# First tokens three weight blocks ahead in the output projection, and the FFN's first weight block done for 128 tokens at a time

## Chip, core and metric

The kernel runs on one core of a Trainium2 chip. The metric is the device time of one execution in microseconds (us); lower is better. Times are the median of several runs. The profile and the trace are of one further execution, whose span (first to last instruction) is a little shorter than its time.

## What is computed

One transformer layer over 256 latent tokens of width 2048 with 256 context tokens. The change concerns the step from the first half of the layer to the second. In the reference:

```
y = (sigmoid(ga) * (oa @ w_br_a) + sigmoid(gb) * (ob @ w_br_b)) @ w_o
x = x + gt1 * rms_norm(y, g_attn_post)
h = modulate(rms_norm(x, g_ffn_pre), sh2, sc2)          # h * (1 + sc2) + sh2
u = depthwise_conv(h @ w_up, conv_w, conv_b)            # w_up: 2048 x 11264
a, g = split(u, 2)
x = x + gt2 * rms_norm((silu(g) * a) @ w_down, g_ffn_post)
```

So the projection `@ w_o` must be complete over all 2048 columns of a token before that token's norm is known, and all of `h` follows from two such norms, one after the other. Between the last product of the projection and the first of the FFN lies a passage of small steps.

## The kernel before

Weights come from HBM in blocks of 128 x 2048 (`raw`, four buffers, loaded by SyncE's queue in one fixed order). `split` makes two float32r halves of each block, a high one on ScalarE (line 127, `wh`) and the rest on VectorE (line 131, `wl`); a block is split in two pieces of 1024 columns. Each product is done as three matmuls, high by high, high by low and low by high. `block()` hands out the next block, splits the one after it and loads further ones.

**The projection** (`norm_gain`, called with `nm="o"`) holds its weights as the moving operand: four column groups `c` of 512, each four blocks deep. Tokens are in two halves, t = 0 (first 128) and t = 1 (the others), with one PSUM tile each, `py_o..0` and `py_o..1`. In the last column group both halves share the first blocks, then the last `lead` = 2 blocks are done for t = 0 first and, with the same weights held, for t = 1. `close(t)` squares and sums the result on ScalarE and multiplies it by a gain on VectorE; `residual(t)` (the argument `done`) takes the norm, adds to `x1`, and takes the second norm's sum of squares. For t = 1 the last 512 columns of `x1` are also made on TensorE, in PSUM (`px`, lines 979 and 985, with a diagonal matrix `dg` of the norm's factor).

**The passage.** `scaled(t, c0, c1)` multiplies feature tiles c0 to c1 of `x1` by the second norm's factor into `yg` (VectorE, or ScalarE with a last argument True). `turn(b, ts)` transposes the feature tiles of group b for the token halves ts on TensorE into the PSUM tile `ptx` b. `split_h2(b)` makes from it the two float32r parts of `h2` for each feature tile j: the high one on ScalarE (line 1043), the low one on VectorE (lines 1047 and 1048; for every fourth j ScalarE does one more pass, line 1042, and VectorE one fewer, line 1045). `keep_busy` issues matmuls whose result nobody uses.

**The FFN's first weight blocks** are laid out so that four output tiles `pu` 0 to 3 grow together over the 16 feature tiles k: `first_pairs(k)` issues for each of the four one matmul of 512 columns (line 174) and one of 256 (line 175). Block `B_UP` holds k = 0 to 3, the next one k = 4 to 7, and so on. Afterwards the FFN goes output tile by output tile.

The order on TensorE is as written in the passage (`manual_schedule`); on the other engines a scheduler sets it, bound by `issue_after`. Each engine runs its instructions in order, and semaphores join the engines. A PSUM tile is used by one engine at a time: where two feature tiles share one `ptx`, ScalarE's read of the second waits for VectorE's read of the first.

## Time and profile before

| | before |
|---|---|
| time, median of 3 runs | 1512.99 us (1512.9 to 1513.67) |
| time of the profiled execution | 1512.95 us |
| its span | 1511.0 us |
| TensorE busy | 1499.6 us, 99% of the span |
| VectorE, ScalarE busy | 1132.4 us (75%), 781.6 us (52%) |
| mean granted TensorE clock | 0.999 of full speed |

TensorE's matmuls are pipelined: a busy engine is one with a matmul in flight, and what one matmul costs is the distance from its start to the next one's start. All starts are in us from the span's start.

### The profile page before, as it was taken

The page shows a single profiled execution, that of the slowest core. Times are in us where ns is not written, and L with a number is a line of the kernel's source. Part 1 is how long each engine was busy: PE and PEld are TensorE (multiplying, and loading weights), DVE is VectorE, ACT ScalarE, POOL GpSimd, SP SyncE. Part 2 cuts the span into 40 slices and gives each one's busy share as a digit, 9 for nine tenths or more (in the row PEclk, how much of TensorE's full clock was granted, in tenths as well). Part 3 has the DMA queues.
Part 4 walks back from the last instruction along what each step waited for, and adds up shares of the span by engine and source line. Part 5 has one row for each costly group of instructions (what it writes and reads, how often), then busy time and mean ns, then how long its engine had stood idle before and what let it go on. Part 6 is the DMA issues. An engine that isn't in the chain of part 4 may idle for free.

```text
span 1511.0 us, 21644 instructions
## 1 busy us (share of the span) xinstructions
PE 1499.6 (99%) x8549; PEld 1289.3 (85%) x8549; DVE 1132.4 (75%) x1679; ACT 781.6 (52%) x1277; POOL 1.6 (0%) x10
## 2 busy tenths in 40 slices
PE   9999999999999999999999999999999999999998
PEld 7876889898888888888888888888888888888886
DVE  4496997999988888877678888788788776444444
ACT  4342542777764455554467555555555555344342
POOL 0000000000000000000000000000000000000000
PEclk9999999999999999999999999999999999999999
DMA  9988779754368888879846676666666556555552
GB/s 368 401 319 335 273 290 341 263 168 168 140 252 294 324 327 308 309 268 356 309 178 226 249 250 220 238 243 236 234 248 232 192 192 257 217 195 195 195 195 84
DMA packets 59253, 381.07 MB, mean 252 GB/s; under 512 B 6544, under 2 KB 6928, under 8 KB 17040
## 3 DMA queue, kind: packets, MB, share of 16 engines
q1 hardware_dynamic: 58432, 378.63, 67.5%
q8 instruction: 67, 1.10, 0.3%
q10 hardware_dynamic: 720, 1.07, 0.2%
q14 instruction: 34, 0.28, 0.1%
HBM read 375.43 MB, written 4.24 MB: 251 GB/s over the span
## 4 chain that ended last, share of the span: by engine, by line
PE 97%; DVE 1%; DMA 1%; ACT 1%; issue 0%; DVEq 0%; ACTq 0%
PE pu L174 21%; PE py_d L883 16%; PE pu L175 11%; PE pv L656 7%; PE pg L174 7%; PE pk L438 7%; PE py_o L883 6%; PE pq L174 4%; PE pb L174 4%; PE pg L175 4%; PE pq L175 2%; PE pb L175 2%; PE s L763 1%; PE po L793 1%; PE pm L312 1%; PE pt L784 1%
## 5 line engine op out<-in xcount | busy, mean ns | idle before, releaser
L131 DVE TENSOR_TENSOR wl<-raw,wh 128x1024 fp32r<-128x1024 f32 x444 | 529.9, 1221 | 222.8 <-ACT wh L127 222.7
L127 ACT ACTIVATE wh<-raw 128x1024 fp32r<-128x1024 f32 x444 | 452.9, 1054 | 294.6 <-PE py_d L883 129.2
L174 PE MATMUL pu<-h,wh 128*128 128x512 f32 x1404 | 488.1, 391 | 0.0
L175 PE MATMUL pu<-h,wl 128*128 128x256 f32 x1404 | 395.9, 282 | 0.0
L174 PEld LDWEIGHTS pu<-h,wh 128*128 128x128 f32 x1404 | 263.6, 188 | 55.6 <-issue 0.4
L175 PEld LDWEIGHTS pu<-h,wl 128*128 128x128 f32 x1404 | 265.4, 189 | 0.0
L883 PE MATMUL py_d<-wh,ff 128*128 128x512 f32 x704 | 216.8, 389 | 0.0
L174 PE MATMUL pg<-h,wh 128*128 128x512 f32 x464 | 161.5, 390 | 0.0
L883 PEld LDWEIGHTS py_d<-wh,ff 128*128 128x128 f32 x704 | 132.1, 188 | 27.6
L204 DVE SCALAR_TENSOR_TENSOR raw<-raw,crb 128x2048 f32<-128x2048 f32 x64 | 146.2, 2285 | 8.8 <-DMA raw<-in_wm_b_dram 8.7
L883 PE MATMUL py_d<-wl,ff 128*128 128x512 f32 x352 | 136.9, 389 | 0.0
L175 PE MATMUL pg<-h,wl 128*128 128x256 f32 x464 | 130.8, 282 | 0.0
L438 PE MATMUL pk<-h,ku 128*128 128x512 f32 x480 | 118.1, 398 | 0.9 <-DVE ku L131 0.4
L179 ACT ACTIVATE half_u<-pu 128x256 f32<-128x256 f32 x88 | 33.5, 383 | 152.7 <-PE pu L175 152.7
L438 PEld LDWEIGHTS pk<-h,ku 128*128 128x128 f32 x480 | 87.5, 188 | 25.6 <-issue 4.8
L174 PE MATMUL pq<-h,wh 128*128 128x512 f32 x304 | 108.6, 395 | 0.0
L174 PEld LDWEIGHTS pg<-h,wh 128*128 128x128 f32 x464 | 87.1, 188 | 18.2
L656 PE MATMUL pv<-wh,h 128*128 128x512 f32 (+1 forms) x384 | 101.8, 354 | 0.0
L174 PE MATMUL pb<-h,wh 128*128 128x512 f32 x256 | 89.4, 390 | 0.0
L175 PEld LDWEIGHTS pg<-h,wl 128*128 128x128 f32 x464 | 87.7, 189 | 0.0
L175 PE MATMUL pq<-h,wl 128*128 128x256 f32 x304 | 85.5, 281 | 0.0
L180 DVE TENSOR_TENSOR u<-pu,half_u 128x256 f32<-128x256 f32 x88 | 37.1, 423 | 56.7 <-ACT half_u L179 56.6
(193 smaller groups left out, 1790.4 us busy)
## 6 DMA issues: line engine op xcount, KB each, us to landing
raw<-in_ws_dram SPq DMA_DIRECT2D x222, 1024.0 KB, 4.8
raw<-in_wm_b_dram SPq DMA_DIRECT2D x64, 1024.0 KB, 4.9
raw<-in_wm_sc_dram SPq DMA_DIRECT2D x15, 1024.0 KB, 7.4
raw<-in_wm_sh_dram SPq DMA_DIRECT2D x16, 768.0 KB, 6.8
raw<-in_wkt_dram SPq DMA_DIRECT2D x10, 1024.0 KB, 5.1
raw<-in_wk_dram SPq DMA_DIRECT2D x7, 768.0 KB, 8.0
crb<-sild SPq DMA_DIRECT2D x5, 1024.0 KB, 6.4
sd<-in_wm_sd_dram SPq DMA_DIRECT2D x4, 1024.0 KB, 8.1
```

The source lines that it names most:

```text
L127: a_ = nc.scalar.activation(hi, src, AF.Copy)
L131: v_ = nc.vector.tensor_tensor(out=lo, in0=src, in1=hi, op=ALU.subtract)
L174: nc.tensor.matmul(pt[:, :], wh[:, w], a, start=first and i == 0, stop=False, skip_group_check=True)
L175: nc.tensor.matmul(pt[:, :S], wl[:, w], a[:, 0], start=False, stop=last and i == n - 1, skip_group_check=True)
L179: a_ = nc.scalar.activation(t[:], pt[:, S:], AF.Copy)
L180: v_ = nc.vector.tensor_tensor(out=out_, in0=pt[:, :S], in1=t[:], op=ALU.add)
L204: nc.vector.scalar_tensor_tensor(out=r, in0=r, scalar=1.0, in1=row, op0=ALU.mult, op1=ALU.mult, accum_out=modx[:, j : j + 1])
L312: nc.tensor.matmul(pm[32 * j : 32 * j + 32, t * P : t * P + P], cc[:, q, :], rsc[k + t][:, q * P : q * P + P], start=q < 4, stop=q >= KT - ...
L438: nc.tensor.matmul(pk[:], wt[:, w], hh[:, :, k, a], start=k == 0 and a == 0 and wt is wh, stop=k == KT - 1 and a == 1)
L656: nc.tensor.matmul(pv[i][:, :nw], src[:, k, a, t0 : t0 + P], wt[:, w], start=k == 0 and q == 0, stop=k == KT - 1 and q == 2)
L763: nc.tensor.matmul(s_ps[:], qs[hd][:, a, qt * P : qt * P + P], k_, start=q == 0, stop=q == 2)
L883: p_ = nc.tensor.matmul(py[t][:], act[:, k, a, t * P : t * P + P], wt[:, w], start=k == 0 and q == 0, stop=k == nk - 1 and q == 2)
```

## The change

In the last column group of the projection `lead` becomes 3, so the first tokens are done three blocks ahead of the others. That needs a third place for split weights: block `B_UP - 2` goes into the second half of `h2`, which is not yet in use, and the half of block `B_UP + 1` that serves k = 4 and 5 is split early into `crt`, the tile of a row that is no longer needed. The other half keeps its place in the passage.

While the others' last block is being done (after the first of its four k), four transposes are put between its matmuls (`ahead(1)`): feature tiles 0 to 3 of the first tokens, in two PSUM tiles `a` and `b`. Their `h2` is made at once, and `close(1)` stands behind it on ScalarE and VectorE.

`half_pairs(k, t)` does the FFN's first weight block (k = 0 to 3) for one token half: for each of the four `pu` one matmul of 2 x 128 columns and one of 128 (or, for k = 0 and t = 1, three of 128). For t = 0 it runs in the passage, two k ahead of the second half of `px` and two behind, in the place of most of `keep_busy`. For t = 1 it runs after the passage, in the place of `first_pairs(0)` to `first_pairs(3)`. `first_pairs` goes on from k = 4. The groups of feature tiles are cut anew: tiles 1 to 3 of the second tokens share one PSUM tile, and from tile 4 on they go in pairs (4, 5), (6, 7) and so on, where before they were (1, 2), (3, 4), (5, 6) and on. The first tokens' transposes of the second norm are all made from `yg`, after `scaled`, where before the first seven were made with a diagonal matrix.

```diff
-    def norm_gain(act, nk, yg, grow, ss, nm, lead, done, extra=None):
+    def norm_gain(act, nk, yg, grow, ss, nm, lead, done, extra=None, ahead=None):
...
-            py = [acc(f"py_{nm}{c}_{t}") for t in range(2)]
+            py, before = [acc(f"py_{nm}{c}_{t}") for t in range(2)], []
...
-            def part(wts, g, t):
+            def part(wts, g, t, between=None):
                 wh, wl = wts
                 for kk in range(4):
+                    if between and kk == 1:
+                        between()
                     k = 4 * g + kk
                     w = slice(kk * 512, kk * 512 + 512)
                     for q, (a, wt) in enumerate(((0, wh), (1, wh), (0, wl))):
...
             def close(t, after=None):
                 with ExitStack() as es:
-                    if after:
-                        es.enter_context(tc.issue_after(after))
+                    for i_ in [after] * bool(after) + before:
+                        es.enter_context(tc.issue_after(i_))
                     nc.scalar.activation(yg[:, t, cs], py[t][:], AF.Square, accum_out=ss[:, t, c : c + 1])
-                nc.vector.tensor_tensor(out=yg[:, t, cs], in0=py[t][:], in1=grow[:, cs], op=ALU.mult)
+                    nc.vector.tensor_tensor(out=yg[:, t, cs], in0=py[t][:], in1=grow[:, cs], op=ALU.mult)
...
                     wts.append(block(3))
                     part(wts[-1], g, 0)
-                for t in range(2):
-                    if t:
-                        for i, g in enumerate(range(n - lead, n)):
-                            part(wts[i], g, 1)
-                    close(t, after)
-                    after = done(t)
+                if ahead:
+                    ahead(0)
+                with ExitStack() as es:
+                    for t in range(2):
+                        if t:
+                            es.enter_context(tc.issue_after(final[0]))
+                            es.enter_context(tc.manual_schedule(engines={mybir.EngineType.PE}))
+                            for i, g in enumerate(range(n - lead, n)):
+                                part(wts[i], g, 1, (lambda: before.extend(ahead(1))) if ahead and i == lead - 1 else None)
+                        close(t, after)
+                        after = done(t)
         return after
...
-        crb = silu_row(yp)
+
+        crt = yp.tile([P, D], F32R, name="crt")
+        crb = crt[:].bitcast(F32)
+        sync.dma_start(out=crb, in_=sild[:KT].rearrange("a b -> (a b)").partition_broadcast(P))
...
+        tail = h2[:, KT // 2 :].rearrange("p k a s -> p (k a s)")
+        place[b0 + B_UP - 2] = (tail[:, :2048], tail[:, 2048:])
         place[b0 + B_UP - 1] = yp
...
+        def half_pairs(k, t, part=0):
+
+
+            ts = slice(t * P, t * P + P)
+            wh, wl = parts[nb_[0]]
+            for i in range(4):
+                w = slice(k % 4 * 512 + i * P, k % 4 * 512 + i * P + P)
+                both = pu[i][:].rearrange("p (a s) -> p a s", a=2)[:, :, ts]
+                if part == 0:
+                    nc.tensor.matmul(
+                        both, wh[:, w], h2[:, k, :, ts], start=k == 0 and t == 0, stop=False, skip_group_check=True)
+                    nc.tensor.matmul(pu[i][:, ts], wl[:, w], h2[:, k, 0, ts], start=False, stop=False, skip_group_check=True)
+                elif part == 1:
+                    for wt in (wh, wl):
+                        nc.tensor.matmul(
+                            pu[i][:, ts], wt[:, w], h2[:, k, 0, ts], start=False, stop=False, skip_group_check=True)
+                else:
+                    nc.tensor.matmul(
+                        pu[i][:, S + t * P : S + t * P + P], wh[:, w], h2[:, k, 1, ts], start=False, stop=False,
+                        skip_group_check=True)
...
-                pu.extend(acc(f"pu0_{i}") for i in range(4))
-                px = pu[3]
-                with tc.issue_after(final[0]):
-                    p_ = nc.tensor.matmul(px[:], ident[:], x1[:, t, c3], start=True, stop=False).ins
-                with tc.issue_after(p_):
-                    b_ = keep_busy(4, "2", pu[0])
-                with tc.issue_after(diagonal(0, t)):
-                    diagonal(1, 0)
-                with tc.issue_after(b_):
-                    p_ = nc.tensor.matmul(px[:], dg[0][:], yg[:, t, c3], start=False, stop=True).ins
+                px = acc("px")
+                nc.tensor.matmul(px[:], ident[:], x1[:, t, c3], start=True, stop=False)
+                dg[0] = yp.tile([P, P], F32, name="dg0")
+                nc.scalar.activation(dg[0][:], ident[:], AF.Copy, scale=r[:, 0, t : t + 1])
+                half_pairs(0, 0)
+                half_pairs(1, 0)
+                p_ = nc.tensor.matmul(px[:], dg[0][:], yg[:, t, c3], start=False, stop=True).ins
...
-                if t and c == 2:
+                if c == (2 if t else 3):
...
             if t == 0:
                 rstd_tok(ss[:, 1, t], r[:, 1, t : t + 1])
+                scaled(0, 0, 4)
                 return a_.ins
             with tc.issue_after(v_.ins), tc.issue_after(a_.ins):
-                return p_, rstd_tok(ss[:, 1, t], r[:, 1, t : t + 1])[0]
-
-        p_, q_ = norm_gain(zz, KT, yg, grow, ss[:, 0], "o", 2, residual, beside)
-        zs.close()
-
-
-        group = [(0,)] + [(j, j + 1) for j in range(1, KT - 1, 2)] + [(KT - 1,)]
+                return p_, rstd_tok(ss[:, 1, t], r[:, 1, t : t + 1])[0], px
...
+        group = {"a": (0, 1), "b": (2, 3), 0: (0,), 1: (1, 2, 3)}
+        group.update({2 + i: (4 + 2 * i, 5 + 2 * i) for i in range(6)})
...
-                ptx[b] = (acc if b % 2 else bank)(f"ptx{b}")
+                ptx[b] = (acc if b in (2, 3, 5, 7) else bank)(f"ptx{b}")
+            n = S if b in range(2, 8) else P
             for t in ts:
...
-                        nc.tensor.matmul(d, x1[:, t, j * P : j * P + P], dg[1][:], start=True, stop=True)
-                    else:
-                        nc.tensor.transpose(d, yg[:, t, j * P : j * P + P], ident[:])
-
-        def split_h2(b):
+                    o = f * n + (t * P if n == S else 0)
+                    nc.tensor.transpose(ptx[b][:, o : o + P], yg[:, t, j * P : j * P + P], ident[:])
...
+        def split_h2(b, *args):
             with ExitStack() as es:
                 for i_ in behind:
                     es.enter_context(tc.issue_after(i_))
-                behind[:] = split_tiles(b)
+                behind[:] = split_tiles(b, *args)
             return behind
...
+        nb_ = [0]
+        t0, t1 = slice(0, P), slice(P, S)
+
+        def ahead(i):
+            if i == 0:
+                nb_[0] = nblk[0]
+                pu.extend(acc(f"pu0_{i}") for i in range(4))
+                r_ = raws[nb_[0] + 1]
+                with tc.issue_after(last[0]), tc.issue_after(last[1]):
+                    split(crt[:, : D // 2], crt[:, D // 2 :], r_[:, : D // 2])
+            else:
+
+                for b in "ab":
+                    turn(b, (0,))
+                for j in range(4):
+                    split_h2("ab"[j // 2], t0, (j,))
+                scaled(0, 4, 8)
+                return behind[:]
+
+        p_, q_, px = norm_gain(zz, KT, yg, grow, ss[:, 0], "o", 3, residual, beside, ahead)
+        zs.close()
...
+        def first_pairs(k):
+
+            wts = (crt[:, : D // 2], crt[:, D // 2 :]) if k in (4, 5) else (wh, wl)
...
+                mm2(pu[i], *wts, h2, k % 4, 1, k, False, k == KT - 1, step=512, off=i * P)
 
         wh, wl = parts[nblk[0]]
         with tc.issue_after(p_), tc.manual_schedule(engines={mybir.EngineType.PE}):
-            for b in range(4):
+            half_pairs(2, 0)
+            half_pairs(3, 0)
+            for b in (2, 3):
                 turn(b, (0,))
-            keep_busy(8, "3", pu[0])
-
-            a_ = nc.scalar.activation(x1[:, 1, 1536:], pu[3][:], AF.Copy)
-            with tc.issue_after(a_.ins), tc.issue_after(q_):
-                scaled(0, 7, 8, True)
-                scaled(0, 8, 12, True)
+            ptx[0] = bank("ptx0")
+            keep_busy(3, "3", ptx[0])
+
+            nc.scalar.activation(x1[:, 1, 1536:], px[:], AF.Copy)
             scaled(1, 0, 1)
             scaled(1, 1, 4)
-            scaled(1, 4, 8)
-            behind[:] = [scaled(1, 8, 12)]
+            behind[:] = [q_, scaled(1, 4, 8)]
             turn(0, (1,))
-            split_h2(0)
+            split_h2(0, t1)
             turn(1, (1,))
-            first_pairs(0, 1)
-            split_h2(1)
+            half_pairs(0, 1, 1)
+            split_h2(1, t1, (1,))
+            half_pairs(0, 1, 2)
+            split_h2(1, t1, (2, 3))
+            half_pairs(1, 1)
             turn(2, (1,))
-            first_pairs(0, 2)
-            queue[nblk[0] + 1] = split_h2(2)[:]
+            split_h2(2)
+            half_pairs(2, 1)
+            turn(3, (1,))
+            queue[nblk[0] + 1] = behind[:]
             block(3)
             behind[:] = last
-            turn(3, (1,))
-            first_pairs(1)
+            with tc.issue_after(behind[0]):
+                behind[0] = scaled(0, 8, 12, True)
+            half_pairs(3, 1)
             split_h2(3)
+            with tc.issue_after(behind[1]):
+                behind[1] = scaled(1, 8, 12)
             with tc.issue_after(behind[0]):
                 behind[0] = scaled(0, 12, 16, True)
-            with tc.issue_after(behind[1]):
-                behind[1] = scaled(1, 12, 16)
-            for k in range(2, KT):
+            for k in range(4, KT):
                 if k % 4 == 0:
                     wh, wl = parts[nblk[0]]
-                b = {5: 4, 7: 5, 8: 6, 10: 7, 12: 8}.get(k)
+                b = {5: 4, 7: 5, 9: 6, 11: 7}.get(k)
                 if b:
                     turn(b, (0, 1))
                     split_h2(b)
-                    if b % 2 == 0:
-                        queue[nblk[0] + 1] = behind[:]
-                        block(3)
+                    if b == 4:
+                        with tc.issue_after(behind[1]):
+                            behind[1] = scaled(1, 12, 16)
+                if k in (5, 9, 12):
+                    queue[nblk[0] + 1] = behind[:]
+                    block(3)
+                    behind[:] = last
                 first_pairs(k)
             for q in range(2):
                 sync.dma_start(out=x1d[:, q], in_=x1[:, q])
```

The change moves instructions at three places. **TensorE at the projection's end.** Before (L883 is the projection, `py_o_1` the second tokens' sum, L979 and L985 make `px` in `pu_3`, L236 is `keep_busy`, L1025 the first tokens' transposes):

```order
L883 MATMUL py_o_1_6901<-wh_6966,zz 128x512 x2
L883 MATMUL py_o_1_6901<-wl_6967,zz 128x512
L979 MATMUL pu_3_7057<-x_6466,ident 128x512 [waits DMAHW4_49]
L236 MATMUL pu_0_7054<-ident 128x128 x4
L985 MATMUL pu_3_7057<-yg,dg_7063 128x512 [waits Activation_49]
L1025 MATMUL ptx_7082<-dg_7065,x_6466 128x128 [waits DMAHW6_49,Activation_49]
```

With the change (L890 is the projection, L1053 a transpose, `ptxa` and `ptxb` the first tokens' tiles 0 to 3, `h_6462` in the first row the weights that lie in `h2`):

```order
L890 MATMUL py_o_1_6901<-h_6462,zz 128x512 x12
L890 MATMUL py_o_1_6901<-wh_6952,zz 128x512 x2
L890 MATMUL py_o_1_6901<-wl_6953,zz 128x512
L1053 MATMUL ptxa<-ident,yg 128x128 [waits DVE_49]
L1053 MATMUL ptxa<-ident,yg 128x128
L1053 MATMUL ptxb<-ident,yg 128x128 x2
L890 MATMUL py_o_1_6901<-wh_6952,zz 128x512 x2
```

Four transposes, the first of which waits for VectorE, now stand in front of the projection's last nine matmuls.

**VectorE after the second norm of the second tokens.** Before (L925 ends the norm's factor, L969 is `scaled`: feature tile 0, tiles 1 to 3, 4 to 7 and 8 to 11; L1047 and L1048 make a low part of `h2`):

```order
L925 RECIPROCAL r<-r 128x1 [waits Activation_49]
L969 TENSOR_SCALAR yg<-x_6466,r 128x128 [waits DVE_49]
L969 TENSOR_SCALAR yg<-x_6466,r 128x384
L969 TENSOR_SCALAR yg<-x_6466,r 128x512 x2
L1047 TENSOR_SCALAR h2t_7109<-h_6462,modx 128x256 [waits Activation_49]
L1048 SCALAR_TENSOR_TENSOR h_6462<-ptx_7082,gcol,h2t_7109 128x256 [waits DVE_49,PE_49]
```

With the change (L1069, L1070 and L1067 make low parts, of tile 3 for the second tokens in the first two rows and then of tiles 4 to 7, L131 splits weights, L982 is `scaled` for tiles 8 to 11):

```order
L1069 TENSOR_SCALAR h2t_128_7179<-h_6462,modx 128x128 [waits Activation_49]
L1070 SCALAR_TENSOR_TENSOR h_6462<-ptx_7155,gcol,h2t_128_7179 128x128 [waits DVE_49]
L1069 TENSOR_SCALAR h2t_0_7193<-h_6462,modx 128x256 [waits Activation_49]
L1070 SCALAR_TENSOR_TENSOR h_6462<-ptx_7136,gcol,h2t_0_7193 128x256 [waits DVE_49,PE_49]
L1069 TENSOR_SCALAR h2t_0_7197<-h_6462,modx 128x256 [waits Activation_49]
L1070 SCALAR_TENSOR_TENSOR h_6462<-ptx_7136,gcol,h2t_0_7197 128x256 [waits DVE_49]
L131 TENSOR_TENSOR wl_7212<-raw_6958,wh_7211 128x1024 [waits Activation_49]
L1069 TENSOR_SCALAR h2t_0_7226<-h_6462,modx 128x256 [waits Activation_49]
L1070 SCALAR_TENSOR_TENSOR h_6462<-ptx_7139,gcol,h2t_0_7226 128x256 [waits DVE_49,PE_49]
L1067 TENSOR_TENSOR h_6462<-h2t_0_7230,h_6462 128x256 [waits Activation_49]
L982 TENSOR_SCALAR yg<-x_6466,r 128x512
L1069 TENSOR_SCALAR h2t_0_7249<-h_6462,modx 128x256 [waits DVE_49,Activation_49]
```

`scaled` for tiles 8 to 11 of the second tokens stood in front of all the low parts; now it stands behind those of tiles 0 to 7 and behind half a weight block.

**TensorE around k = 4 and 5.** Before (L174 and L175 are `first_pairs`, k = 4 ahead of the transposes L1027 and k = 5 behind them):

```order
L174 MATMUL pu_3_7057<-h_6462,wh_7145 128x512
L175 MATMUL pu_3_7057<-h_6462,wl_7146 128x256
L1027 MATMUL ptx_7197<-ident,yg 128x128 [waits PE_49]
L1027 MATMUL ptx_7197<-ident,yg 128x128 x3
L174 MATMUL pu_0_7054<-h_6462,wh_7145 128x512 [waits DVE_49,Activation_49]
```

With the change (L179 and L180 are `first_pairs`, L1053 the transposes of tiles 8 and 9, first tokens, then second):

```order
L179 MATMUL pu_3_6995<-h_6462,crt 128x512
L180 MATMUL pu_3_6995<-h_6462,crt 128x256
L1053 MATMUL ptx_7244<-ident,yg 128x128 [waits Activation_49]
L1053 MATMUL ptx_7244<-ident,yg 128x128
L1053 MATMUL ptx_7244<-ident,yg 128x128 [waits DVE_49]
L1053 MATMUL ptx_7244<-ident,yg 128x128
L179 MATMUL pu_0_6992<-h_6462,crt 128x512
```

The transposes of tiles 8 and 9 for both token halves stand between k = 4 and k = 5 as before (there they were of tiles 7 and 8), but the third of them now waits for VectorE, whose work for it is the L982 row above.

## Rows read from the trace of the kernel before

**Rows 1.** The page: busy time by engine, and the chain that ended last.

```profile
PE 1499.6 (99%) x8549; PEld 1289.3 (85%) x8549; DVE 1132.4 (75%) x1679; ACT 781.6 (52%) x1277; POOL 1.6 (0%) x10
...
PE 97%; DVE 1%; DMA 1%; ACT 1%; issue 0%; DVEq 0%; ACTq 0%
```

**Rows 2.** Stretches: length, busy us of each engine (instructions), clock, DMA.

```profile
765.20:772.60 7.40, 6.73 (x46) 5.32 (x44) 5.58 (x15) 6.08 (x18) 0.00 (x0) 1.00 0.51 215
772.60:798.00 25.40, 25.37 (x155) 22.36 (x155) 20.91 (x37) 17.25 (x28) 0.00 (x0) 1.00 0.44 164
798.00:1268.00 470.00, 470.00 (x2709) 416.43 (x2708) 374.05 (x554) 272.07 (x434) 0.00 (x0) 1.00 0.63 227
1503.60:1507.80 4.20, 0.00 (x0) 0.00 (x0) 3.45 (x6) 0.98 (x3) 0.00 (x0) 1.00 0.35 134
1507.90:1511.00 3.10, 0.00 (x0) 0.00 (x0) 0.00 (x0) 0.00 (x0) 0.00 (x0) 0.50 0.51 194
```

**Rows 3.** Timeline of TensorE: start, us, then the instruction; the passage.

```profile
759.78 0.62 PE L883 MATMUL py_o<-wh,zz 128*128 128x512 f32 x2
...
765.22 1.02 PE L979 MATMUL pu<-x,ident 128*128 128x512 f32 x2
...
767.39 1.12 PE L985 MATMUL pu<-yg,dg 128*128 128x512 f32 x2 [0.26 <-ACT dg L962]
768.35 1.72 PE L1025 MATMUL ptx<-dg,x 128*128 128x128 f32 x14
769.91 1.95 PE L236 MATMUL pu<-ident 128*128 128x128 f32 x16
771.70 0.49 PE L1027 MATMUL ptx<-ident,yg 128*128 128x128 f32 x3
772.63 0.39 PE L1061 MATMUL pu<-h,wh 128*128 128x256 f32 x1 [0.44 <-ACT h L1043]
```

**Rows 4.** Timeline of VectorE and ScalarE: the norms of both token halves.

```profile
759.98 0.60 ACT L892 ACTIVATE yg<-py_o 128x512 f32<-128x512 f32 x1 [3.65 <-PE py_o L883]
...
761.50 2.74 DVE L988 SCALAR_TENSOR_TENSOR x<-yg,r,x 128x512 f32<-128x512 f32 x4
...
765.42 0.60 ACT L892 ACTIVATE yg<-py_o 128x512 f32<-128x512 f32 x1
...
766.93 0.69 ACT L962 ACTIVATE dg<-ident,r 128x128 f32<-128x128 f32 x2 [0.50 <-DVE r L925]
...
769.04 0.69 DVE L994 SCALAR_TENSOR_TENSOR yg<-x 128x512 f32<-128x512 f32 x1
...
770.85 1.41 DVE L969 TENSOR_SCALAR yg<-x,r 128x128 f32<-128x128 f32 x4
```

**Rows 5.** Timeline of ScalarE and VectorE: the parts of `h2`, tiles 0 to 7.

```profile
772.01 1.02 ACT L1043 ACTIVATE h<-ptx,modx,gcol 128x256 fp32r<-128x256 f32 x2 [0.49 <-PE ptx L1027]
...
776.40 0.35 DVE L1047 TENSOR_SCALAR h2t<-h,modx 128x256 f32<-128x256 f32 x1
...
777.34 2.36 DVE L131 TENSOR_TENSOR wl<-raw,wh 128x1024 fp32r<-128x1024 f32 x2
...
780.08 0.48 DVE L1048 SCALAR_TENSOR_TENSOR h<-ptx,gcol,h2t 128x256 fp32r<-128x256 f32 x1
780.60 0.56 ACT L1043 ACTIVATE h<-ptx,modx,gcol 128x256 fp32r<-128x256 f32 x1 [1.88 <-DVE h L1048]
781.58 0.48 DVE L1048 SCALAR_TENSOR_TENSOR h<-ptx,gcol,h2t 128x256 fp32r<-128x256 f32 x1
781.99 0.48 DVE L969 TENSOR_SCALAR yg<-x,r 128x512 f32<-128x512 f32 x1
782.71 0.43 DVE L1045 TENSOR_TENSOR h<-h2t,h 128x256 fp32r<-128x256 f32 x1 [0.25 <-ACT h L1043]
```

**Rows 6.** Timeline of TensorE: transposes before k = 5, its start, the first blocks' end.

```profile
780.29 0.60 PE L1027 MATMUL ptx<-ident,yg 128*128 128x128 f32 x4
780.71 0.47 PE L174 MATMUL pu<-h,wh 128*128 128x512 f32 x1
...
797.65 0.39 PE L174 MATMUL pu<-h,wh 128*128 128x512 f32 x1
797.88 0.28 PE L175 MATMUL pu<-h,wl 128*128 128x256 f32 x1
798.00 0.39 PE L174 MATMUL pu<-h,wh 128*128 128x512 f32 x1
```

More of the change, by code (lines that the diff above doesn't have):

```diff
@@ L132, in split, with halves @@
         return a_.ins, v_.ins
[L134 removed]
+    def halves(r, off, pool=None, after=None, first=0):
         n = r.shape[-1]
         b = 1 if pool else 2
[L137 to L140 removed]
+        if isinstance(pool, tuple):
+            h, lo = pool
+        else:
+            h, lo = (
+                (pool or wp).tile([P, 2048 + 128], F32R, tag=f"w{q}", bufs=b, name=f"w{q}{nraw[0]}")[:, off : off + 2048]
+                for q in "hl")
+        for q in (slice(0, n // 2), slice(n // 2, n))[first:]:
             last[:] = split(h[:, q], lo[:, q], r[:, q], after)
@@ L159, in split_to @@
             if q not in parts:
-                parts[q] = halves(raws[q], 8 if q - b0 < B_Q else 0, place.get(q), queue.get(q))
+                parts[q] = halves(
+                    raws[q], 8 if q - b0 < B_Q else 0, place.get(q), queue.get(q), int(q == b0 + B_UP + 1))
     def block(ahead=2, split=True):
@@ L1053, in first_pairs @@
-        def first_pairs(k, part=0):
-            for i in range(4):
-                w = slice(k % 4 * 512 + i * P, k % 4 * 512 + i * P + P)
-                if part == 0:
-                    mm2(pu[i], wh, wl, h2, k % 4, 1, k, False, k == KT - 1, step=512, off=i * P)
-                elif part == 1:
-                    for q, wt in enumerate((wh, wl)):
-                        nc.tensor.matmul(pu[i][:, :S], wt[:, w], h2[:, k, 0], start=q == 0, stop=False, skip_group_check=True)
-                else:
-                    nc.tensor.matmul(pu[i][:, S:], wh[:, w], h2[:, k, 1], start=False, stop=False, skip_group_check=True)
+        nb_ = [0]
```

48 lines of the change are left out of this document (20 added, 28 removed).

## The prediction

> **What bounds the kernel now.** I began with the page: TensorE has a matmul in flight for 99% of the span, and the chain that ended last is 97% TensorE [rows 1]. So a microsecond more or less on TensorE, anywhere, is a microsecond of the time, as long as nothing later has slack. The stretches say where slack is left: behind the first weight blocks the FFN runs 470.00 us with TensorE busy for all 470.00 of them, so whatever the passage loses or gains arrives at the end unchanged [rows 2]. What is to be had lies in the passage, 765.2 to 772.6. Its rows show real work (the two halves of `px`, the first tokens' transposes) and fillers, 16 of them from 769.91 to 771.70 [rows 3]. In the stretch behind it, 772.6 to 798.0, TensorE is busy for 25.37 of 25.40 us, but VectorE is too for 20.91 [rows 2]: it feeds TensorE there with little to spare. That is the number that I kept in mind.
>
> **Prices.** The last 24 matmuls of the projection take 759.78 to 765.22, 0.227 us each for 512 columns; fourteen transposing matmuls take 768.35 to 769.91, 0.111 each [rows 3]. In `first_pairs` a matmul of 512 columns takes 0.23 and one of 256 takes 0.12, so a whole k (four of each) 1.39 [rows 6]. A float32r matmul of 128 columns stands in no row. The bounds are 0.06 (half of 256 columns) and 0.22 (twice the plain float32 rows' 0.111). I take 0.11, since those rows are the only ones of 128 columns.
>
> **Step 1, the projection's end: +1.2 us.** With three blocks held back, 36 matmuls (8.16 us) stand behind the first tokens' last one, which therefore ends at 757.06 instead of 759.78. Their `close` follows 0.20 later, as before, and the adds of the residual end 4.26 later, at 761.52 (759.98 to 764.24) [rows 4]. Then come a square on VectorE, the norm's factor and `scaled`; the same steps of the second tokens take 1.81 us from start to `scaled` (769.04 to 770.85) [rows 4], and `scaled` of 512 columns takes 0.48 [rows 5]. So the four new transposes can begin at about 763.9. TensorE reaches them after 27 of its 36 matmuls, at 763.18. It waits 0.7 us with the projection's last nine matmuls behind it; the transposes add 0.44. The projection ends at 766.4 instead of 765.22.
>
> The third block held, and the half block split into `crt`, cost nothing that I can see: ScalarE stood idle for 3.65 us in front of the first `close` [rows 4], and the block that goes into `h2` need not wait for a buffer, so these splits move into earlier idle time. If that cover were missing, the first `close`, and all behind it, would slip by as much as the half's split takes, about 1.2 us (half of 2.36) [rows 5]. SyncE's queue has the same order as before. The raw buffer of block `B_UP + 1` comes free about 2 us later, and the block that takes its place is due only after the first blocks.
>
> **Step 2, the second tokens' `close`: another +1.2.** It now stands behind the four first-token tiles on both ScalarE and VectorE. How long such a tile takes is read where two share a PSUM tile: ScalarE idles 1.88 us until VectorE is done with the one (780.56), starts at 780.60, and VectorE ends the second at 782.06, so 1.50 us for a tile of 256 columns [rows 5]. For 128 columns no row exists; it lies between 0.75 (half) and 1.50. I take 1.1, since the two hand-overs and the fixed part of three instructions do not shrink. From 764.35 three such tiles and ScalarE's part of the fourth bring the second `close` to 767.8; before it began at 765.42 [rows 4]. With 0.75 it would be 766.8, with 1.50 about 769.
>
> **Step 3, up to the second tokens' first tile: +2.0 in all.** `scaled` follows the `close` by 5.43 us (765.42 to 770.85) [rows 4], now at 773.25. TensorE has its own queue until then: from 766.4, `px` in two parts of 0.96 (767.39 to 768.35) [rows 3], 32 matmuls of `half_pairs` at 0.115 (3.7), four transposes, six fillers (0.7), and about 0.6 of waiting for `dg`, which is ready 1.86 us after the `close` (766.93 plus half of 0.69) [rows 4]. That ends at 773.7. ScalarE's first tile follows by 0.31 (771.70 to 772.01) [rows 3, 5], at 774.0, where before it stood at 772.01. What the change wanted out of the passage, half of the work of k = 0 to 3, is done by now, but 2.0 us later than the passage ended before.
>
> **Step 4, the wait ahead of k = 5: +2.5.** This is the largest term. The transposes of tiles 8 and 9 need `scaled` of tiles 8 to 11, which on VectorE has moved from in front of all low parts to behind those of tile 7. I add up the chain from 774.0. Tiles 0 to 3 of the second tokens, three of them in one PSUM tile: 4.3 (four whole tiles with one such hand-over took 772.01 to 776.40, 4.4). Tile 4: 0.94 (776.40 to 777.34). Tile 5, waiting for tile 4: 1.50. Half a weight block: 1.18 (half of 2.36). Tile 6: 0.9. Tile 7, whose two passes on ScalarE (1.02 together) wait for tile 6, with VectorE's 0.43 behind: 1.5. `scaled`: 0.48. All from [rows 5]. Together 10.8, so the third transpose starts at 784.9 and k = 5 at 785.2. Before, it started at 780.71 [rows 6], 8.70 after the first tile. On TensorE there is meanwhile only the second tokens' 36 half matmuls (4.1), four transposes (0.4) and k = 4 (1.4); it arrives at about 780.6 and waits some 4.2 us, with two transposes in the middle. Sum so far: 785.2 - 780.7 = +4.5.
>
> **Step 5, from k = 5 on: +0.5.** Eleven k as before (780.71 to 798.00 with everything between) [rows 6], two transposes fewer (-0.2). VectorE leaves step 4 with all of tiles 8 to 15 and two and a half weight blocks still to do, pairs again one behind the other: up to the first half of the weights of k = 12 that is about 12 us (tiles 8 to 13 at 0.94 and 1.5 in turn, three halves at 1.18, `scaled`, and some waiting), against some 11 of TensorE's work. I put 0.7 for waits there.
>
> **Sum.** +4.5 + 0.5 = +5.0 on the profiled execution's 1512.95 (span 1511.0 and some 2 us around it; it stands at the median of the runs, 1512.99): **1518.0 us**. The price of the 128-column matmul hardly enters: at 0.06 TensorE only waits longer for VectorE, and at 0.22 part of its 40 x 0.11 = 4.4 more falls into waits, for about +7.3 in all. With tiles of 0.75 the sum is about +3.6, with tiles of 1.50 about +7.4.
>
> **Rivals.**
> *VectorE keeps up, and TensorE's own work decides (the other side).* From 766.4 TensorE has `px` 1.9, the first weight block in halves 7.8, twelve k 16.7, 27 transposes 3.0 and fillers 0.7, in all 30.1: the first blocks end at 796.5 instead of 798.0. That is -1.5, 1511.4 us, no change that can be measured; faster only if a 128-column matmul costs 0.06, which takes off another 40 x 0.05 = 2.0 to 2.2 (1509.3). It decides once the chain of step 4 is under about 6.5 us instead of 10.8. For it speaks that four of the chain's eight tiles are half as wide; against it that VectorE's own work in that chain, without any hand-over, comes to 6.3 to 7.9 us (four tiles at half or all of 0.83, three at 0.83, then 0.43, 1.18 and 0.48, all [rows 5]), and that the hand-over stands in a row. I give it 0.07, of which 0.03 for the cheap matmul.
> The Trainium skill speaks against that cheap matmul: "TensorE: Matmul & The Clock Gate", section "LDWEIGHTS (loading the stationary operand)", has the load of the weights take a time set by their columns alone, which makes about 0.107 us for 128, so that fewer moving columns save nothing. By that rule, as an estimate, this rival ends at 1511.4; by halving it ends at 1509.3. The fourteen transposes at 0.111 agree, though they are plain float32.
>
> *The waits are half as long.* Shorter tiles and better overlap take 1 us from step 2 and 2 from step 4: +1.5 to +2.5, about 1515.0. For it: no row has a tile of 128 columns. Against: in step 4 only the first 4.3 us hang on those. 0.17.
>
> *Longer still.* The tile near 1.50, or the matmul near 0.22: 1520.3. Or the clock falls in the wait of step 4: after TensorE's last matmul the granted clock stayed at 1.00 through 1507.80 and was 0.50 (1.2 instead of 2.4 GHz) behind that [rows 2], after 4.2 us without a matmul; here a like wait has two transposes in it, so I expect it to hold. A fall for 3 us would cost 1.5 us more. Together 0.16.
>
> That the change does not do what it says is excluded by the order of instructions.
>
> **How the numbers follow.** The forecast (1516.5 to 1519.5) gets 0.60. A measurement of this kernel can tell about 0.2% (3.0 us) from no change. Faster by more than that: 0.04. Within it: the rest of the first rival and most of the second, 0.21. Slower: 0.75. The range runs from the second rival, 1514.5, to the third, 1521.0; outside lie the first rival and a little on either end.
>
> **What would show it.** In the trace after: four transposes inside the projection with an idle TensorE of about 0.7 us ahead of them, and the last projection matmul ending near 766.4; the second `close` near 767.8; a first-token tile of 128 columns near 1.1 us; the third transpose of tiles 8 and 9 released by VectorE's `scaled` after an idle TensorE of 3 to 4 us; k = 5 near 785; the first blocks' end near 803. The prediction is wrong if that wait is under 1.5 us, or if the projection still ends by 765.7.

## The result: 0.34% slower

The changed kernel takes 1518.04 us (median of 6 runs, 1517.62 to 1519.22), the kernel before 1512.91 in the same job (6 runs): a ratio of 1.0034, 95% interval 1.0022 to 1.0047. The profiled execution took 1517.62 us, with a span of 1515.8. From the projection's first matmul to the kernel's last it is 829.87 us in the trace; before it was 825.01. So 4.9 us are lost between the two, and the windows say where. Windows of the changed kernel (columns as in [rows 2]):

```profile
766.50:774.70 8.20, 7.63 (x54) 6.12 (x52) 6.59 (x19) 5.25 (x15) 0.00 (x0) 1.00 0.19 79
774.70:803.00 28.30, 24.96 (x153) 22.19 (x153) 18.87 (x37) 16.70 (x27) 0.00 (x0) 0.94 0.45 163
803.00:1273.00 470.00, 470.00 (x2708) 417.03 (x2707) 374.55 (x554) 272.13 (x434) 0.00 (x0) 1.00 0.63 226
781.00:784.40 3.40, 0.44 (x2) 0.20 (x2) 2.21 (x5) 2.20 (x5) 0.00 (x0) 1.00 0.43 118
784.60:787.60 3.00, 3.00 (x10) 2.61 (x11) 0.95 (x3) 1.28 (x3) 0.00 (x0) 0.50 0.45 188
```

The FFN is as full as before. In the first blocks TensorE is idle for 3.3 of 28.3 us, all of it ahead of k = 5, and there is something that the kernel before did not have there: 3 us of full work at half the granted clock (0.50, that is 1.2 instead of 2.4 GHz). TensorE's timeline of the changed kernel:

```profile
759.96 2.97 PE L890 MATMUL py_o<-h,zz 128*128 128x512 f32 x12
762.76 0.63 PE L890 MATMUL py_o<-wh,zz 128*128 128x512 f32 x2
763.23 0.40 PE L890 MATMUL py_o<-wl,zz 128*128 128x512 f32 x1
763.79 0.44 PE L1053 MATMUL ptxa<-ident,yg 128*128 128x128 f32 x2 [0.17 <-DVE yg L982]
...
766.37 1.02 PE L1011 MATMUL px<-x,ident 128*128 128x512 f32 x2
...
769.70 1.13 PE L1016 MATMUL px<-yg,dg 128*128 128x512 f32 x2 [0.51 <-ACT dg L1013]
...
774.58 0.28 PE L998 MATMUL pu<-h,wl 128*128 128x128 f32 x1
774.69 0.27 PE L998 MATMUL pu<-h,wh 128*128 128x128 f32 x1
...
776.12 0.33 PE L993 MATMUL pu<-h,wh 128*128 128x256 f32 x1
776.28 0.22 PE L995 MATMUL pu<-h,wl 128*128 128x128 f32 x1
776.34 0.34 PE L993 MATMUL pu<-h,wh 128*128 128x256 f32 x1
...
781.17 0.44 PE L1053 MATMUL ptx<-ident,yg 128*128 128x128 f32 x2 [0.36 <-ACT yg L981]
784.58 0.69 PE L1053 MATMUL ptx<-ident,yg 128*128 128x128 f32 x2 [2.98 <-DVE yg L982]
784.92 0.78 PE L179 MATMUL pu<-h,crt 128*128 128x512 f32 x1
...
787.63 0.48 PE L179 MATMUL pu<-h,wh 128*128 128x512 f32 x1
...
802.92 0.39 PE L179 MATMUL pu<-h,wh 128*128 128x512 f32 x1
```

k = 5 starts at 784.92 (before 780.71 [rows 6]) and takes 2.71 us to the start of k = 6 at 787.63. ScalarE and VectorE of the changed kernel:

```profile
764.26 0.46 ACT L1065 ACTIVATE h<-ptxa,modx,gcol 128x128 fp32r<-128x128 f32 x1 [1.25 <-PE ptxa L1053]
765.53 0.46 ACT L1065 ACTIVATE h<-ptxa,modx,gcol 128x128 fp32r<-128x128 f32 x1 [0.81 <-DVE h L1070]
...
767.38 0.46 ACT L1065 ACTIVATE h<-ptxb,modx,gcol 128x128 fp32r<-128x128 f32 x1 [1.04 <-DVE h L1070]
767.74 0.59 ACT L899 ACTIVATE yg<-py_o 128x512 f32<-128x512 f32 x1
...
773.90 0.46 ACT L1065 ACTIVATE h<-ptx,modx,gcol 128x128 fp32r<-128x128 f32 x1 [1.01 <-PE ptx L1053]
```
```profile
783.70 0.43 DVE L1067 TENSOR_TENSOR h<-h2t,h 128x256 fp32r<-128x256 f32 x1 [1.09 <-ACT h L1065]
784.04 0.48 DVE L982 TENSOR_SCALAR yg<-x,r 128x512 f32<-128x512 f32 x1
```

The second `close` starts at 767.74 behind the fourth first-token tile, and VectorE idles 1.09 us ahead of its subtraction for tile 7, right in front of the late `scaled`.

### The profile page after: what moved, and what is told of

Read it like the earlier page. It is cut to its first block, busy times and chain, and to the rows that moved or that the text cites. A ratio compares the mean times of both kernels' runs of the same rounds, so it can differ in the third digit from the quotient of the medians.

```text
span 1515.8 us, 21665 instructions
## 1 busy us (share of the span) xinstructions
PE 1501.1 (99%) x8556; PEld 1291.5 (85%) x8556; DVE 1135.5 (75%) x1692; ACT 781.0 (52%) x1276; POOL 1.6 (0%) x10
## 4 chain that ended last, share of the span: by engine, by line
PE 96%; DVE 2%; DMA 1%; ACT 1%; issue 0%; DVEq 0%; ACTq 0%
PE pu L179 21%; PE py_d L890 16%; PE pu L180 11%; PE pv L661 7%; PE pg L179 7%; PE pk L443 7%; PE py_o L890 5%; PE pq L179 4%; PE pb L179 4%; PE pg L180 4%; PE pq L180 2%; PE pb L180 2%; PE s L768 1%; PE po L798 1%; PE pm L317 1%; PE pt L789 1%
## 5 line engine op out<-in xcount | busy, mean ns | idle before, releaser
L131 DVE TENSOR_TENSOR wl<-raw,wh 128x1024 fp32r<-128x1024 f32 x441 | 526.5, 1221 | 216.2 <-ACT wh L127 216.0
L179 PE MATMUL pu<-h,wh 128*128 128x512 f32 x1384 | 480.4, 391 | 0.0
L180 PE MATMUL pu<-h,wl 128*128 128x256 f32 x1384 | 390.8, 282 | 0.0
L179 PEld LDWEIGHTS pu<-h,wh 128*128 128x128 f32 x1384 | 260.0, 188 | 53.8
L180 PEld LDWEIGHTS pu<-h,wl 128*128 128x128 f32 x1384 | 262.5, 190 | 0.0
L890 PE MATMUL py_d<-wh,ff 128*128 128x512 f32 x704 | 217.0, 390 | 0.0
L179 PE MATMUL pg<-h,wh 128*128 128x512 f32 x464 | 161.5, 391 | 0.0
L890 PEld LDWEIGHTS py_d<-wh,ff 128*128 128x128 f32 x704 | 132.1, 188 | 27.3
L209 DVE SCALAR_TENSOR_TENSOR raw<-raw,crb 128x2048 f32<-128x2048 f32 x58 | 132.5, 2287 | 11.8 <-DMA raw<-in_wm_b_dram 11.5
L890 PE MATMUL py_d<-wl,ff 128*128 128x512 f32 x352 | 137.1, 390 | 0.0
L180 PE MATMUL pg<-h,wl 128*128 128x256 f32 x464 | 131.0, 282 | 0.0
L179 PE MATMUL pq<-h,wh 128*128 128x512 f32 x304 | 108.6, 396 | 0.0
L179 PEld LDWEIGHTS pg<-h,wh 128*128 128x128 f32 x464 | 87.2, 188 | 18.0
L179 PE MATMUL pb<-h,wh 128*128 128x512 f32 x256 | 89.4, 391 | 0.0
L180 PEld LDWEIGHTS pg<-h,wl 128*128 128x128 f32 x464 | 87.9, 189 | 0.0
L180 PE MATMUL pq<-h,wl 128*128 128x256 f32 x304 | 85.6, 282 | 0.0
```

The costliest lines, as they stand in the source:

```text
L131: v_ = nc.vector.tensor_tensor(out=lo, in0=src, in1=hi, op=ALU.subtract)
L179: nc.tensor.matmul(pt[:, :], wh[:, w], a, start=first and i == 0, stop=False, skip_group_check=True)
L180: nc.tensor.matmul(pt[:, :S], wl[:, w], a[:, 0], start=False, stop=last and i == n - 1, skip_group_check=True)
L209: nc.vector.scalar_tensor_tensor(out=r, in0=r, scalar=1.0, in1=row, op0=ALU.mult, op1=ALU.mult, accum_out=modx[:, j : j + 1])
L890: p_ = nc.tensor.matmul(py[t][:], act[:, k, a, t * P : t * P + P], wt[:, w], start=k == 0 and q == 0, stop=k == nk - 1 and q == 2)
```

## Experiments

A kernel's whole effect is best read from the projection's first matmul to the kernel's last in its one profiled execution, since what comes ahead of that varies by up to 2 us. What comes behind the first blocks does not vary: from the start of the next output tile (802.92 in the changed kernel, 798.00 before) to the last matmul all eleven traces take 705.17 us. So a difference in the last column arises in the projection and the first blocks.

| kernel | median us | ratio to before (95%) | first projection matmul to last matmul, us |
|---|---|---|---|
| before | 1513.24 | | 825.01 |
| changed | 1518.04 | 1.0034 (1.0022 to 1.0047) | 829.87 |
| early `scaled` | 1517.23 | 1.0025 (1.0015 to 1.0035) | 828.57 |
| fillers in the wait | 1517.24 | 1.0030 (1.0019 to 1.0041) | 829.43 |
| before, lead = 3 | 1513.17 | 1.0003 (0.9994 to 1.0012) | 825.26 |
| before, late `scaled` | 1514.70 | 1.0012 (1.0003 to 1.0021) | 826.51 |
| odd tile first | 1516.94 | 1.0024 (1.0014 to 1.0034) | 829.11 |
| both | 1513.60 | 1.0003 (0.9994 to 1.0012) | 825.85 |
| both, weights first | 1514.05 | 1.0003 (0.9995 to 1.0012) | 826.09 |
| the same, early `close` | 1513.37 | 1.0000 (0.9991 to 1.0009) | 825.27 |
| all | 1512.97 | 0.9999 (0.9990 to 1.0008) | 824.73 |

(Before: 26 runs in the job of the four rows from the early `scaled` on and 30 in that of the next four, 1513.24 in both; 15 runs and 1513.07 in that of the last row; 6 runs and 1512.91 in that of the changed kernel. The ratio is not the quotient of the medians.)

**1. The early `scaled`.** The diff shows VectorE's part; `scaled(0, 8, 12)` on ScalarE goes back to its early place in the same way.

```diff
-            behind[:] = [q_, scaled(1, 4, 8)]
+            scaled(1, 4, 8)
+            behind[:] = [q_, scaled(1, 8, 12)]
...
-            with tc.issue_after(behind[1]):
-                behind[1] = scaled(1, 8, 12)
```

> The changed kernel with the two `scaled` of columns 8 to 11 given back their early place: scaled(1, 8, 12) right behind scaled(1, 4, 8) on VectorE, ahead of all low parts of the second tokens, and scaled(0, 8, 12) on ScalarE right behind its copy of px. Nothing else is changed. My theory: the wait ahead of k = 5 (4.3 us of the 4.9 that the first blocks end later) hangs on that place alone. The third transpose of tiles 8 and 9 then starts about 780.7 instead of 784.58, the granted clock stays at 1.00 there, k = 5 takes 1.39 us instead of 2.71, and, less a few tenths of new waits for low parts, the time is 1513.3 to 1514.3 us. The second tokens' first tile is 0.3 to 0.5 us later, since one more `scaled` of 0.48 us may stand ahead of it. Rival: the chain of low parts on VectorE and the shared PSUM tiles are the bound, and the wait only moves to a later transpose or matmul; then the time is 1516 us or more, with an idle TensorE of over 2 us somewhere between 775 and 790.

The rival holds: 1517.23 us. The wait ahead of k = 5 is gone (k = 5 starts at 781.08), and others stand at k = 8 and k = 12 instead. TensorE, then VectorE of this kernel:

```profile
787.38 0.50 PE L179 MATMUL pu<-h,wh 128*128 128x512 f32 x1 [1.09 <-ACT wh L127]
788.87 0.39 PE L180 MATMUL pu<-h,wl 128*128 128x256 f32 x1 [0.99 <-DVE wl L131]
...
796.21 0.38 PE L180 MATMUL pu<-h,wl 128*128 128x256 f32 x1 [0.62 <-DVE wl L131]
```
```profile
783.77 0.43 DVE L1067 TENSOR_TENSOR h<-h2t,h 128x256 fp32r<-128x256 f32 x1 [1.09 <-ACT h L1065]
784.84 0.36 DVE L1069 TENSOR_SCALAR h2t<-h,modx 128x256 f32<-128x256 f32 x1 [0.64 <-ACT h L1065]
...
787.60 2.35 DVE L131 TENSOR_TENSOR wl<-raw,wh 128x1024 fp32r<-128x1024 f32 x2
```

k = 8 waits for both parts of its weights, 2.1 us, and k = 12 again for 0.6 (2.5 and 0.8 by the distances between starts). VectorE is no faster: it still idles 1.09 us for tile 7 and 0.64 for tile 8, and comes to the weights too late. So the moved instruction decided where TensorE waited, but the trace is only 1.3 us shorter without the move.

**2. Fillers in the wait.**

```diff
+                    if b == 4:
+                        ptx[4] = bank("ptx4")
+                        keep_busy(12, "4", ptx[4])
                     turn(b, (0, 1))
```

> The changed kernel with 24 filler matmuls of 128 columns (about 2.7 us) ahead of the transposes of tiles 8 and 9, inside the wait in front of k = 5, in which TensorE did nothing for 3.2 us at a stretch. They write a PSUM tile that the transposes write afterwards, so nothing of the result changes. My theory: the granted clock stays at 1.00 from 784.4 to 787.8, where it was 0.50; k = 5 takes 1.39 us instead of 2.71 and starts no later; the time falls by about 1.4 us, to 1516.6. Rival: the fall costs nothing, since VectorE's low parts and the weights would bound the stretch from k = 5 to k = 8 anyway and the time saved is waited for at k = 8; then 1518.0 us, with a new idle TensorE of over 1 us at k = 7 or k = 8.

Timeline of TensorE in this kernel:

```profile
784.45 0.44 PE L1053 MATMUL ptx<-ident,yg 128*128 128x128 f32 x2 [0.88 <-DVE yg L982]
784.64 0.48 PE L179 MATMUL pu<-h,crt 128*128 128x512 f32 x1
...
786.12 0.39 PE L179 MATMUL pu<-h,wh 128*128 128x512 f32 x1
...
796.91 0.39 PE L180 MATMUL pu<-h,wl 128*128 128x256 f32 x1 [0.65 <-DVE wl L131]
```

```profile
784.60:786.10 1.50, 1.50 (x10) 1.34 (x10) 0.47 (x2) 0.57 (x1) 0.00 (x0) 1.00 0.71 295
```

The clock holds (second fence, a window of this kernel, columns as in [rows 2]) and k = 5 takes 1.48 us instead of 2.71. But of the 1.23 us 0.8 are waited for at k = 12 (0.65 idle in the row, 0.81 by the starts), where the changed kernel had no wait, and 0.44 us arrive at the end of the trace. Each theory was half right. The medians can't tell this kernel from the changed one.

**3. and 4. One part of the change alone, on the kernel before.** Three blocks held back (`lead` = 3 in the call of `norm_gain`, the third block in `h2`'s tail), and the late `scaled`:

```diff
-            scaled(1, 4, 8)
-            behind[:] = [scaled(1, 8, 12)]
+            behind[:] = [scaled(1, 4, 8)]
...
             split_h2(3)
+            with tc.issue_after(behind[1]):
+                behind[1] = scaled(1, 8, 12)
```

> The kernel before with one part of the change alone: three weight blocks instead of two are held back for the first tokens at the end of the projection (the third one's two halves stand in the second half of h2). My theory: the first tokens' close moves 2.7 us earlier, but the second tokens' close still stands right behind TensorE's last matmul of the projection, and all of the passage hangs on that; so the time is that of the kernel before, 1512.7 to 1513.3 us. Rival: holding a third block back costs something by itself (the later release of buffers, the split of the third block in front of the first close), then 1514 us or more, and part of the 5.1 us has to be looked for there.

> The kernel before with one part of the change alone, the late place of scaled(1, 8, 12): on VectorE behind the low parts of the tiles ahead of the fourth transposed group instead of in front of all low parts. My theory: TensorE then waits for it ahead of k = 5, by about 2 us, the first blocks end about 2 us later, and the time is about 1515 us (1514.3 to 1515.8); the wait is too short for the clock to fall. Rival: the place does not matter where the work in front of it is the same in sum, since VectorE has as much to do until k = 8 either way; then 1513.0 us.

Both as my theory had it. The third block neither gains nor costs anything that the runs can tell; its trace is 0.25 us longer, and 0.24 of that lies in the projection: the 24 matmuls whose weights lie in `h2` start 0.234 us apart, those of the block behind them, in `yp`, 0.230, instead of 0.227. The late `scaled` costs 1.5 us in the kernel before. TensorE there, and a window behind the wait, in which the clock has held:

```profile
783.08 0.33 PE L1027 MATMUL ptx<-ident,yg 128*128 128x128 f32 x1 [1.74 <-DVE yg L969]
```
```profile
783.20:784.60 1.40, 1.40 (x9) 1.24 (x10) 0.26 (x2) 1.09 (x3) 0.00 (x0) 1.00 0.86 363
```

**5. and 6. The odd tile first, without and with the early `scaled`.** After the first run I had a new theory: VectorE's whole chain bounds the stretch, and the new pairs lengthen it. Before, tiles 3, 7 and 11, which ScalarE does in two passes, stood first in their pair, and VectorE's subtraction read no PSUM; now tiles 7, 11 and 15 stand second in theirs, and each waits for its neighbour (tile 3 of the second tokens is done in one pass now).

```diff
             n = ts.stop - ts.start
-            for f, j in enumerate(group[b]):
+            both = list(enumerate(group[b]))
+            for f, j in both[::-1] if b in (3, 5, 7) else both:
```

> The changed kernel; in the pairs of tiles (6, 7), (10, 11) and (14, 15), which share a PSUM tile, the odd one is taken first. ScalarE makes both of its parts from PSUM and VectorE only subtracts, without reading PSUM, so ScalarE need not wait for VectorE between the two; in the changed kernel each of these pairs has such a wait (1.0 to 1.2 us of idle VectorE ahead of its 0.43 us subtraction). The place of scaled(1, 8, 12) is left late. New theory (VectorE's chain as a whole is the bound from 774 on, and these hand-overs are a part of it): scaled ends about 0.8 us earlier, so k = 5 starts near 784.1 instead of 784.9; the pair (10, 11) gives a further microsecond ahead of the weights of k = 12; the time falls to 1516 to 1517.2 us, the lower end if the shorter wait keeps the clock at 1.00. Rival (only the place of scaled and the clock count): k = 5 moves by 0.8 us and nothing else, and the idle time returns at k = 8; 1517.5 us or more.

> The early scaled (as in the first run, where the waits moved to the weights of k = 8, 2.5 us, and of k = 12, 0.8 us) together with the odd tile first in the three pairs. If VectorE's chain is the bound, the wait at k = 8 falls by the one hand-over ahead of it (2.5 to about 1.4 us), the one at k = 12 disappears, and k = 6 waits 0.3 us longer, since tile 6 is now second: 1515.2 us (1514.8 to 1515.8). Rival: something else makes the weights late (the transfer of the raw block, ScalarE's half of the split); then the waits at k = 8 and k = 12 stay and the time is 1517 us as with the early scaled alone.

Alone it brings 0.76 us in the trace: k = 5 starts 0.73 earlier, but the wait in front of it is still 2.30 us and the clock falls all the same. TensorE, and two windows, of the kernel with the odd tile first alone:

```profile
783.85 0.69 PE L1053 MATMUL ptx<-ident,yg 128*128 128x128 f32 x2 [2.30 <-DVE yg L982]
```
```profile
784.30:786.30 2.00, 2.00 (x9) 1.71 (x8) 0.84 (x2) 0.71 (x2) 0.00 (x0) 0.50 0.74 311
786.90:802.00 15.10, 15.10 (x93) 13.48 (x93) 11.82 (x19) 9.47 (x14) 0.00 (x0) 1.00 0.57 208
```

The two together bring 4.0 us, where one by one they bring 1.30 and 0.76: the early `scaled` alone moved TensorE's wait to the weights, and the odd tile first alone left it with the late `scaled`. I had expected 1515.2 and measured 1513.60. One edit takes out two hand-overs, as VectorE (first fence) and TensorE of that kernel show (all starts of this trace are 1.9 us later, since its projection begins at 680.15 instead of 678.22):

```profile
783.67 0.42 DVE L1068 TENSOR_TENSOR h<-h2t,h 128x256 fp32r<-128x256 f32 x1
...
784.95 0.35 DVE L1070 TENSOR_SCALAR h2t<-h,modx 128x256 f32<-128x256 f32 x1
```
```profile
785.09 0.47 PE L179 MATMUL pu<-h,wh 128*128 128x512 f32 x1 [0.47 <-DVE h L1071]
788.98 0.39 PE L180 MATMUL pu<-h,wl 128*128 128x256 f32 x1 [0.21 <-DVE wl L131]
```

The 1.09 us ahead of the subtraction and the 0.64 ahead of tile 8 are both gone; of the waits at k = 8 and k = 12 there is 0.21 left, and k = 6 waits 0.47 for the tile that is now second.

**7. and 8. Weights ahead of tiles 8 and 9; then the second `close` ahead of the fourth first-token tile.** The first in the loop over k; for the second `ahead` makes three tiles instead of four, and the fourth, with ScalarE doing two passes, follows the norm's root:

```diff
                 if b:
                     turn(b, (0, 1))
+                if k == 5:
+                    queue[nblk[0] + 1] = behind[:]
+                    block(3)
+                    behind[:] = last
+                if b:
                     split_h2(b)
...
-                if k in (5, 9, 12):
+                if k in (9, 12):
```
```diff
-                for j in range(4):
+                for j in range(3):
...
-            rstd_tok(ss[:, 0, t], r[:, 0, t : t + 1])
+            a_, v_ = rstd_tok(ss[:, 0, t], r[:, 0, t : t + 1])
...
             if t:
+                with tc.issue_after(a_), tc.issue_after(v_):
+                    split_tiles("b", t0, (3,))
```

> As the one with early scaled and the odd tile first, and the weight block of k = 8 to 11 is split ahead of tiles 8 and 9 instead of behind them. VectorE then ends the first half of the weights about 784.2 and tile 8 about 786.2, when TensorE arrives at k = 8 (786.1); the wait there falls from about 1.4 us to a few tenths, and 0.4 us are waited at k = 9 for the last scaled and 0.3 at k = 12. If VectorE's order of work is all that is left: 1514.3 to 1515.0 us. Rival (VectorE has too much to do in all, whatever its order): the wait goes to k = 9 to k = 12 and the time stays at that of the one before, 1515.2 us or more.

> As the one with the weights first, and the second tokens' close no longer stands behind the fourth of the first tokens' tiles: that tile is taken behind the norm's square root on ScalarE, with one subtraction on VectorE. The close then begins about 766.6 instead of 767.74 (0.2 us behind TensorE's last matmul of the projection), dg and the second half of px are no longer waited for (0.55 us), and the second tokens' first tile starts at 773.0 to 773.2 instead of 773.9; all of VectorE's chain behind it is as much earlier: 1513.5 to 1514.3 us, 0.7 to 0.9 under the one before. Rival: the first tile is held by TensorE's own queue and the added subtraction, and starts no earlier than 773.7; then within 0.2 us of the one before.

The weights first change nothing: 826.09 against 825.85 us, the wait at k = 8 is now one for its tile (0.26 us). The rival there was right that the order changes nothing, though the wait did not go to k = 9 to 12 and both kernels end lower than it said. The early `close` brings 0.8 us in the trace (0.7 in the medians, within the runs' scatter): `dg` is no longer waited for, and counted from the projection's first matmul the `close` begins 1.16 us earlier than in the changed kernel and the second tokens' first tile 0.74.

**9. All order repaired.**

> As the one with the early close, with what its trace still showed of waits in the first blocks taken out by order alone: the first tokens' transposes stand two k later in the projection's last block (0.33 us of wait there), no fillers ahead of the second tokens' first tile (0.78), the two scaled of the second tokens' columns 4 to 11 on VectorE stand in idle time between low parts instead of ahead of them, the weight block of k = 8 to 11 and that of k = 12 to 15 are split in two halves with the pair of tiles between them, and k = 7 goes ahead of k = 6 and k = 11 ahead of k = 10, as their tiles are made. If the waits were all that kept the halved passage from its gain, TensorE has nothing to wait for from 774 on, the last transposes and k = 15 end 1 to 1.8 us earlier than in that run, and the time is 1511.6 to 1512.6 us, under the kernel before (1513.2). Rival: TensorE's own work was the bound by then (matmuls of 128 columns at 0.11 each, so halving a k costs 0.43 us), or VectorE is still late somewhere; then 1513 us or more.

The core of the edit (`late` issues `scaled` behind the low part just made; a hook in `halves` puts the pair of tiles between the two halves of a block; `kk == 2` puts the first tokens' transposes one k later, not two as the text above has it):

```diff
-                    if between and kk == 1:
+                    if between and kk == 2:
...
-            keep_busy(3, "3", ptx[0])
...
             split_h2(0, t1)
+            late(1, 4, 8)
...
             split_h2(1, t1, (1,))
+            late(1, 8, 12)
...
-            for k in range(4, KT):
+            for k in (4, 5, 7, 6, 8, 9, 11, 10, 12, 13, 14, 15):
```

1512.97 us, the same as before (1513.07). What TensorE still waits for:

```profile
773.18 0.87 PE L1058 MATMUL ptx<-ident,yg 128*128 128x128 f32 x4 [0.49 <-DVE yg L984]
775.90 0.35 PE L995 MATMUL pu<-h,wh 128*128 128x256 f32 x1 [0.29 <-DVE h L1076]
795.34 0.47 PE L181 MATMUL pu<-h,wh 128*128 128x512 f32 x1 [0.25 <-DVE h L1076]
```

That is 1.0 us in all. My theory had the place of the waits but not the gain: even without any of them this passage would, by estimate, be about 1.3 us under the kernel before (0.28 in the trace and these 1.0; 1.7 with the waits by the starts, 1.45), if they came out in full, which no run shows. That is about the size of the effect of the fourth run, at the edge of what the medians can tell.

## Why the prediction was right, and where a step was off

In the trace the first tile of the second tokens starts 1.9 us later (predicted 2.0), from there to k = 5 it is 2.3 us more (2.5), and behind that 0.7 (0.5): 4.9 us instead of 5.0. The steps one by one:

- **Step 1** (projection ends at 766.4): 766.37. One term was too large and one was missing: the wait was 0.33 us instead of 0.7 (763.23 to 763.79, less 0.235 for the matmul itself), and the slower projection matmuls, which I had not foreseen, added about 0.25 (the third run has 0.24). The two make up for each other, since slower matmuls bring TensorE later to the transposes; the transposes themselves start at 763.79, where I had 763.9.
- **Step 2** (`close` at 767.8): 767.74. The first three tiles take 1.27 us and then 1.85 for two (764.26, 765.53, 767.38), 1.04 each in the mean, 1.1 estimated; only those that share a PSUM tile pay the hand-over. The eighth run takes 1.16 us of this back at the `close`, and 0.8 arrive at the end.
- **Step 3** (first second-token tile at 774.0): 773.90.
- **Step 4** (k = 5 at 785.2, after a wait of about 4.2): 784.92, after waits of 0.36 and 2.98 us (0.53 and 3.14 by the starts) with two transposes between them. The chain that I added up was the right one, down to the hand-over of tile 7 (1.5). What I gave as its cause, the place of `scaled`, holds only in part: the first run shows 1.3 of 4.9 us for it, and takes ScalarE's `scaled` back with VectorE's. The regrouping of the pairs, which my sum contained as "1.5" per second tile without naming it a change, is the other part; the sixth run shows 4.0 for both.
- **Step 5** (+0.5 from k = 5 on): the number is near (18.00 us to 802.92, before 17.29 [rows 6], so +0.7), the reason was wrong, so the number is luck. No weight was waited for. Instead k = 5 ran at half the clock and took 1.2 us more than the 1.51 of before (780.71 to 782.22 there), which left VectorE time for the weights. I had put the fall among the rivals and expected the clock to hold; the second run shows that the two, fall and weights, largely stand for each other: without the fall, 0.8 of its 1.23 us return as a wait for weights.
- **The price of 128 columns** (0.11): 0.11 alone (774.58 to 774.69), and 0.23 for a pair of 256 and 128 columns (776.12 to 776.34, and in the mean of such pairs), against 0.35 for a whole pair [rows 6]: a k in two halves costs 0.44 us more than in one piece. The fourteen rows of 0.111 that I took the price from are seven tiles, two rows for each plain float32 matmul; that float32r would cost one such row and not two was a guess that came out. The price is what kept the first rival's gain small, and the last run, with the waits nearly gone, bears it out: 0.28 us under the kernel before. The Trainium skill, "TensorE: Matmul & The Clock Gate", section "LDWEIGHTS (loading the stationary operand)", has the weight load set by its columns alone, by estimate 0.107 us for 128. The distance of 0.11 from start to start agrees, but the trace lists each such load with 0.19 us, overlapping its neighbours, so that the load sets the price is not shown.

## What to carry to other kernels

When a stage is fed by an engine with little to spare, undoing one suspect at a time may only move the waits (here 1.3 and 0.8 us one by one, 4.0 together); count the feeder's idle gaps up to the next block of weights, and repair those together. Where two tiles share a PSUM tile, put the one whose second engine reads no PSUM first. Before a passage is filled with halves of later work, price the halves: where 128 columns cost as much as 256 (0.11 and 0.12 us here), they can use up most of what the idle time was worth, as in the last run.

## What I had not expected of the hardware

The clock fell to 0.50 in the wait although two transposes stood in it (0.44 us busy in 781.0 to 784.4), and stayed there through 3 us of full work; it fell again in the wait of 2.30 us of the fifth run, and did not in the kernel before with the late `scaled`, which waited 1.74.

The projection matmuls of 512 columns with weights in `h2` start 0.234 us apart (twelve from 759.96 to 762.76), those of the block behind, in `yp`, 0.230 in the third run, and all others 0.227. In the kernel before the block in `yp` has 0.227 as well (759.78 to 765.22 [rows 3]), so that buffer alone is not the reason; no run here tells what is.
